# Rounding weight tiles one tile ahead, dealing whole tiles, and decay matrices by pairs of heads, in a hybrid DeltaNet and Conformer block

## The chip, the cores and the metric

The kernel runs on one core of one Trainium2 chip. The metric is the device time of one execution in microseconds, the median over several runs. The core has a matrix engine (PE; its weight loads are listed apart as PEld), VectorE (DVE), ScalarE (ACT), GpSimd (POOL) and SyncE (SP, which here issues most transfers). Each engine takes its instructions in a fixed order and waits at an instruction until the data of that instruction is there.

## The reference, cut to what matters

The block has 512 frames of width 1024, all in float32. One projection `h @ w_in` of the normalised input gives everything that the first stage needs: q, k, v and z of 8 heads of width 128, two small columns per head for the decay and for beta, the two halves of a gated linear unit, and two gates.

```python
h = rmsnorm(x, norm1_w[l])
proj = h @ w_in[l]
q, k, v, z, b_raw, a_raw, glu, gates = jnp.split(proj, SPLITS, axis=-1)
qkv = silu(causal_depthwise_conv(concat([q, k, v]), dn_conv_w[l]))     # 4 taps
q, k = l2norm(q), l2norm(k)
o = gated_delta_rule_chunked(q, k, v, g, beta)                         # per head
out_a = (rmsnorm(o, dn_norm_w[l]) * silu(z)) @ dn_w_o[l]
c = ga * sigmoid(gb)                                                   # glu
c = silu(layernorm(causal_depthwise_conv(c, cm_dw_w[l]) + cm_dw_b[l])) # 31 taps
out_b = c @ cm_w_pw2[l] + cm_b_pw2[l]
x = x + (sigmoid(gate_a) * out_a + sigmoid(gate_b) * out_b) @ w_out[l]
x = x + (silu(f_gate) * f_up) @ ffn_w_down[l]        # f_gate, f_up of rmsnorm(x)
```

The delta rule needs, for each head and chunk of frames, the matrix `decay = exp(gc_i - gc_j)` for j not above i and zero elsewhere, where `gc` is a running sum of the decay logarithms. It multiplies both `k k^T` and `q k^T`.

## The kernel before, in words

**Products.** Every float32 operand of a large product is split into two halves in PE's fast format, a rounded one and the rest. ACT makes the rounded one (`whi`, a copy, line 111) and DVE the rest (`wlo`, a subtraction, line 112). `split3` (line 121) then issues three matmuls for each 128 rows: `whi` with the high half of the activations, `whi` with the low half, and `wlo` with the high half. A weight tile is 128 x 1024; the product of one tile with all 512 frames takes 24 matmuls of 128 x 512 and gives one PSUM bank. `unit` (lines 101 to 113) loads a tile from memory over SP into `raw`, and makes `whi` and `wlo`; each of the three names has three buffers.

**The stage.** Of the 64 tiles of `w_in`, four are multiplied early. The other sixty run in a loop of generators. `proj(j)` (line 393) calls `unit` for tile j and then issues its eight groups of three matmuls, one group a step, into a bank of the pool `mm`, which has three. `head(h)` (line 793) runs the tiles 8+h (k), h (q), 16+h (v) and 24+h (z), 32 steps; head 0's k and q run interleaved in `proj2`, from tiles loaded before. For q, k and v, `conv4` (line 415) follows the tile: ACT scales the bank by the last tap into `acc` (line 419; the name `acc4` has two buffers), DVE adds three more taps (line 422), and ACT applies Silu (line 425) into `kT`, `qT` or `vT`. z goes through Silu straight from its bank (line 812). Between heads, `take(OTHERS[h])` runs so many steps of the other projections: `glu(i)` takes tile 40+i, a Sigmoid on ACT (line 677) and tile 32+i, for i from 2 to 7, and `gate(i)` takes tile 48+i and a Sigmoid (line 705). A tile is eight steps, so 12 steps are one and a half tiles. What is left of the others runs after the last head.

**Each head's recurrence.** `front` (line 451) transposes k, squares it on ACT, multiplies k by k, scales the result on ACT into `Un`, and multiplies it on POOL by the decay matrix `DT`; small blocks of that go through memory (`sc`, `U`) into a solve of thirty short POOL instructions. `front2` (line 507) transposes v and q and multiplies q by k; DVE multiplies that by `DT` into `at`. `chain` (line 529) finishes the inverse and runs over the four chunks of frames; it begins at a step of its own for each head, `START - 9 + 32 h + sum(OTHERS[:h])`, and is spread over some 65 steps beside the tiles of the next head.

**Decay matrices.** `decays` (line 773), traced at the third step of the loop, makes the running sums, with three small Exps, and stores a row per head and chunk in memory (`mrow`). `decay(*heads)` (line 438) does three things for each head: SP loads that row broadcast over 128 partitions into `DT` (four buffers, line 442), POOL adds a mask of large negative numbers (line 444), and ACT applies four Exps (line 449), one a chunk. It is called for head 0 in `decays`, for head 1 in head 0, and for heads 2 and 3, 4 and 5, 6 and 7 in heads 1, 3 and 5.

**What sets the order.** The framework's planner fixes the order of each engine's instructions before the run: at each point of its own forecast it takes, among those that it holds ready, the one that was traced first (the 31-tap convolution of the other branch, on DVE, ranks far behind and fills gaps). `tc.issue_after(i)` queues what its block traces on the engine of `i` behind `i`, in order alone. `marked` remembers the last instruction of a kind on each engine, `behind()` queues a block behind these marks, and both roundings of a tile are marked as "unit". The functions Silu, Sigmoid and Exp need different tables on ACT; a load of a table is placed by the compiler where the function changes, and shows as ACT_TABLE_LOAD under the line of the function that needs it.

From step 335 on, each call of `unit` also calls `fill`, which issues a part of the copies and sums that the FFN stage will read.

Of the kernel before, what the change touches and what calls it, by code (L numbers as in the profile page):

```python
# [6 lines left out]
F32 = mybir.dt.float32  # L7
F32R = mybir.dt.float32r
I32 = mybir.dt.int32
AF = mybir.ActivationFunctionType  # L10
ALU = mybir.AluOpType
# [3 lines left out]
P = 128  # L15
T = 512
NT = 4
D = 1024
KD = 8
H = 8  # L20
# [4 lines left out]
START = 78  # L25
ROUND = 40
WARM = 9
OTHERS = (12, 12, 12, 12, 8, 8, 8, 8)
EPS = 1e-6


# [1 line left out]
def block_kernel(ctx, tc, a):  # L33
    nc = tc.nc
    V, S, G, PE = nc.vector, nc.scalar, nc.gpsimd, nc.tensor
# [49 lines left out]
    def marked(b, kind="drain"):  # L85
        mark[b.ins.engine, kind] = b.ins
        return b
# [10 lines left out]

    last = [None]

    def unit(ap, pool=None):

        aps = ap if isinstance(ap, tuple) else (ap,)
        n = T * len(aps) if isinstance(ap, tuple) else 1024
        raw, hi, lo = ((pool or wp).tile([P, n if pool else 1024], t, name=x)[:, 0:n]
                       for t, x in ((F32, "raw"), (F32R, "whi"), (F32R, "wlo")))
        for i, p in enumerate(aps):
            loads.append(nc.sync.dma_start(raw[:, i * T:(i + 1) * T] if len(aps) > 1 else raw, p))
        if start_feed[0]:
            fill()  # L110
        marked(S.activation(hi, raw, AF.Copy), "unit")  # L111
        marked(V.tensor_tensor(out=lo, in0=raw, in1=hi.bitcast(F32), op=ALU.subtract), "unit")  # L112
        return hi, lo

    def split3(ps, wt, xh, xl, first, last, mv=False):

        wh, wl = wt
        terms = ((wh, xh), (wh, xl), (wl, xh))
        for i, (w, m) in enumerate(terms):
            l, r = (m, w) if mv else (w, m)  # L120
            marked(PE.matmul(ps, l, r, start=first and i == 0, stop=last and i == 2))  # L121
# [268 lines left out]
    def even_odd(t):  # L390
        return t.rearrange("p (q e) c -> p e q c", e=2)

    def proj(j):

        ps = psm.tile([P, T], F32, name="mm")
        hi, lo = unit(a["win"][j])
        for k in range(KD):
            s = slice(k * P, (k + 1) * P)
            if k:
                yield  # L400
            split3(ps, (hi[:, s], lo[:, s]), hh[:, k, :], hl[:, k, :], k == 0, k == KD - 1)
        return ps

    def proj2():

        both = [(psm.tile([P, T], F32, name="mm"), u) for u in first_two]
        for k in range(KD):
            s = slice(k * P, (k + 1) * P)
            for i, (ps, (hi, lo)) in enumerate(both):
                if k or i:  # L410
                    yield
                split3(ps, (hi[:, s], lo[:, s]), hh[:, k, :], hl[:, k, :], k == 0, k == KD - 1)
        return [ps for ps, _ in both]

    def conv4(j, name, ps=None):
        if ps is None:
            ps = yield from proj(j)
        acc = tp.tile([P, T], F32, name="acc4")
        S.activation(acc, ps, AF.Copy, scale=c4w[:, j, 3:4])  # L419
        for k in (2, 1, 0):  # L420
            s = 3 - k
            marked(V.scalar_tensor_tensor(out=acc[:, s:], in0=ps[:, :T - s], scalar=c4w[:, j, k:k + 1],  # L422
                                          in1=acc[:, s:], op0=ALU.mult, op1=ALU.add))
        o = gp.tile([P, NT, P], F32, name=name, bufs=1 if name == "vT" else 3)
        marked(S.activation(o.rearrange("p n t -> p (n t)"), acc, AF.Silu))
        yield
        return o

# [6 lines left out]
            PE.transpose(ps[:, n, :], src[:, n, :], ident)  # L435
        return ps

    def decay(*heads):

        for h in heads:  # L440
            DT = gp.tile([P, NT, P], F32, name="DT", bufs=4)
            nc.sync.dma_start(DT.rearrange("p n t -> p (n t)"),
                              mrow[h].rearrange("n t -> (n t)").partition_broadcast(P))
            G.tensor_tensor(out=DT, in0=DT, in1=neg.rearrange("p (a t) -> p a t", a=1).broadcast_to([P, NT, P]),
                            op=ALU.add)
            dts.append(DT)
        for h, DT in zip(heads, dts[-len(heads):]):
            for n in range(NT):
                S.activation(DT[:, n, :], DT[:, n, :], AF.Exp, bias=nmc[:, n, h:h + 1])

    def front(h, kT, DT):
        sq = junk[:, 0:P]
# [298 lines left out]
    def close():  # L751

        if ended and count[0] - ended[0][0] > ROUND - 8:
            if ended[0][1]:
                finish(*ended.pop(0)[2])
            else:
                scaled(*ended[0][2])
                ended[0][1] = True
# [14 lines left out]
    def decays():  # L773

        yield 2
        gps = psg.tile([P, 4, P], F32, name="g")
        fl = lambda t: t.rearrange("p n h -> p (n h)")
        for i, m in enumerate((tri, suf, ones, mid)):
            PE.matmul(gps[:, i, 0:32], m, fl(g), start=True, stop=True)
        S.activation(fl(egc), gps[:, 0, 0:32], AF.Exp)  # L780
        S.activation(fl(kdf), gps[:, 1, 0:32], AF.Exp)
        S.activation(fl(egl), gps[:, 2, 0:32], AF.Exp)
        V.tensor_scalar(out=negc, in0=egc, scalar1=-1.0, scalar2=None, op0=ALU.mult)
        V.tensor_scalar(out=fl(nmc), in0=gps[:, 3, 0:32], scalar1=-1.0, scalar2=None, op0=ALU.mult)
        mps = psg.tile([P, 4, P], F32, name="g")
        PE.matmul(mps[0:32, 0, :], fl(g), mid, start=True, stop=True)
        mr = mrt[0:32, 0:P]
        S.activation(mr, mps[0:32, 0, :], AF.Copy)
        for n in range(NT):
            nc.sync.dma_start(mrow[:, n, :], mr[n * H:(n + 1) * H])  # L790
        decay(0)

    def head(h, done):

        pk, pq = (yield from proj2()) if h == 0 else (None, None)
        k_ = yield from conv4(8 + h, "kT", pk)
        close()
        q_ = yield from conv4(h, "qT", pq)
        close()
        v = conv4(16 + h, "vT")  # L800
        for _ in range(2):
            next(v)
            yield
        DT = dts.pop(0)
        if h == 0 or h % 2 and h + 1 < H:
            decay(*range(h + 1, h + 3 if h else 2))
        with behind(), tc.issue_after(last[0].ins) if h else nullcontext():
            ss, kd, b2, Un, cp, y = front(h, k_, DT)
        v_ = yield from v
        pz = yield from proj(24 + h)  # L810
        z_ = zall[:, h, :]
        S.activation(z_, pz, AF.Silu)


        def second():
            Vp, at = front2(k_, q_, v_, DT, ss)
            done.append((h, k_, q_, ss, kd, b2, Un, cp, Vp, at, y, z_))
            yield 0

        chains.append([count[0] + 5, second()])  # L820
        yield
# [10 lines left out]
            yield  # L832


    done, ended, dts, convs, count, chains = [], [], [], [], [0], [[0, decays()]]
    rest = others()
    for h in range(H):
        queue.append(head(h, done))
# [241 lines left out]
    ff, made = [], []  # L1080
# [308 lines left out]
```

## Time and profile before

| | before |
|---|---|
| median of 3 runs | 942.55 us (942.53 to 944.67) |
| profiled execution | 943.44 us, its span 941.7 us |
| PE busy | 925.4 us, 98% of the span |
| DVE busy | 740.8 us, 79% |
| ACT busy | 558.0 us, 59% |
| POOL busy | 336.8 us, 36% |
| the loop of `proj` tiles | about 34 to 461 us |

Times in the profile are microseconds from the start of the span; in the groups of instructions the last number of a duration is the mean in ns. A line of a timeline gives the start, the duration, the engine and line, the operation, what it writes and reads, how many like it follow each other, and in brackets how long the engine had been idle and what ended that. Matmuls overlap, so their pace is read from one start to the next and not from the duration. A line of the table by stretches gives the stretch, its length, the busy time of PE, PEld, DVE, ACT and POOL with the count of instructions, the granted clock of PE as a share of the full one, and the transfers' share and rate.

### The profile page before, as it was taken

The numbers are of one execution on the slowest core, as the hardware profiler recorded it, in microseconds if no ns is written. First come the engines' busy times: TensorE is split into PE (matmuls) and PEld (weight loads), VectorE is DVE, ScalarE is ACT, GpSimd is POOL, SyncE is SP. The second block draws the span as 40 slices with busy tenths as digits, with TensorE's granted clock in tenths as the row PEclk, the third lists the DMA queues.
The fourth block names the chain that finished last, engine by engine and source line by source line (L and its number), as shares of the span: only waits on it lengthen the run. The fifth ranks groups of instructions, "written<-read, shape, count | busy, mean of one in ns | idle before, by whom it ended". The sixth has DMA issues, their size and how long they took to land.

```text
span 941.7 us, 14545 instructions
## 1 busy us (share of the span) xinstructions
PE 925.4 (98%) x4952; PEld 785.3 (83%) x4952; DVE 740.8 (79%) x1157; ACT 558.0 (59%) x1278; POOL 336.8 (36%) x541
## 2 busy tenths in 40 slices
PE   9999999999999999999999999999999999999996
PEld 6777788878888888888888888988889999988885
DVE  4889898989989899999587643676536877888896
ACT  6696977888778796643555323324324445466545
POOL 0134345253353437544055341245531111133042
PEclk9999999999999999999999999999999999999999
DMA  9333413223123246989898983699797564577654
GB/s 322 113 114 118 131 68 103 86 85 108 73 77 103 93 136 159 335 263 268 284 286 279 285 236 127 205 292 288 257 257 213 184 197 168 186 236 255 213 181 148
DMA packets 78187, 177.39 MB, mean 188 GB/s; under 512 B 10080, under 2 KB 19472, under 8 KB 77088
## 3 DMA queue, kind: packets, MB, share of 16 engines
q1 hardware_dynamic: 66528, 144.89, 44.9%
q0 software_dynamic: 10288, 28.90, 13.3%
q10 hardware_dynamic: 1296, 2.67, 0.7%
q8 instruction: 39, 0.64, 0.3%
q14 instruction: 36, 0.29, 0.1%
HBM read 156.22 MB, written 45.37 MB: 214 GB/s over the span
## 4 chain that ended last, share of the span: by engine, by line
PE 82%; ACT 7%; DVE 3%; issue 1%; POOL 1%; DMA 1%; POOLq 0%; ACTq 0%; DVEq 0%; SPq 0%
PE mm L121 55%; PE w L121 20%; PE b L526 2%; DVE wlo L112 1%; ACT whi L111 1%; PE g L435 1%; PE g L470 1%; PE st L639 1%; PE st L630 1%; PE st L638 1%; PE st L624 1%; PE st L625 0%; ACT Un L473 0%; DVE xs L964 0%; PE b L435 0%
## 5 line engine op out<-in xcount | busy, mean ns | idle before, releaser
L111 ACT ACTIVATE whi<-raw 128x1024 fp32r<-128x1024 f32 (+1 forms) x191 | 196.4, 1030 | 242.6 <-PE mm L121 158.0
L112 DVE TENSOR_TENSOR wlo<-raw,whi 128x1024 fp32r<-128x1024 f32 (+1 forms) x191 | 239.6, 1256 | 86.1 <-ACT whi L111 84.8
L121 PE MATMUL mm<-hh,whi 128*128 128x512 f32 (+1 forms) x688 | 269.7, 392 | 1.2 <-ACT whi L111 0.8
L121 PE MATMUL mm<-hh,wlo 128*128 128x512 f32 (+1 forms) x688 | 264.2, 385 | 0.8 <-DVE wlo L112 0.8
L121 PE MATMUL mm<-hl,whi 128*128 128x512 f32 (+1 forms) x688 | 263.0, 382 | 0.0
L693 DVE SCALAR_TENSOR_TENSOR cps<-c,c31w,cps 128x512 f32<-128x512 f32 x224 | 167.9, 749 | 3.8
L121 PEld LDWEIGHTS mm<-hh,wlo 128*128 128x128 f32 x688 | 130.0, 189 | 25.0 <-DVE wlo L112 1.3
L121 PEld LDWEIGHTS mm<-hh,whi 128*128 128x128 f32 x688 | 130.3, 189 | 22.9 <-ACT whi L111 1.7
L121 PEld LDWEIGHTS mm<-hl,whi 128*128 128x128 f32 x688 | 130.3, 189 | 20.9
L1022 POOL TENSOR_TENSOR fm<-fm 128x256 f32<-128x256 f32 x33 | 28.1, 852 | 117.7 <-DVE s L1022 93.2
L422 DVE SCALAR_TENSOR_TENSOR acc<-mm,c4w,acc 128x511 f32<-128x511 f32 (+2 forms) x72 | 53.0, 740 | 4.3 <-ACT acc L419 4.1
L502 POOL TENSOR_TENSOR ytm<-U,y 128x60 f32<-128x60 f32 (+14 forms) x120 | 36.7, 306 | 51.0 <-DMA U<-sc 42.2
L121 PE MATMUL mm<-yh,whi 128*128 128x512 f32 x128 | 50.6, 396 | 0.0
L121 PE MATMUL mm<-yh,wlo 128*128 128x512 f32 x128 | 49.8, 389 | 0.0
L121 PE MATMUL mm<-yl,whi 128*128 128x512 f32 x128 | 49.8, 389 | 0.0
L121 PE MATMUL w<-hh,wlo 128*128 128x256 f32 x168 | 47.7, 284 | 0.3 <-DVE wlo L112 0.3
L121 PE MATMUL w<-hh,whi 128*128 128x256 f32 x168 | 47.6, 284 | 0.0
L121 PE MATMUL w<-hl,whi 128*128 128x256 f32 x168 | 47.5, 283 | 0.0
L196 POOL DMA_DIRECT2D s<-in_wgu_dram x24 | 22.7, 962 | 64.0 <-DMA s<-in_wgu_dram 64.0
L121 PE MATMUL w<-wlo,fh 128*128 128x512 f32 (+1 forms) x115 | 44.3, 385 | 0.2 <-DVE wlo L112 0.2
L121 PE MATMUL w<-whi,fl 128*128 128x512 f32 (+1 forms) x115 | 44.2, 385 | 0.0
L121 PE MATMUL w<-whi,fh 128*128 128x512 f32 (+1 forms) x115 | 44.2, 385 | 0.0
(346 smaller groups left out, 1937.5 us busy)
## 6 DMA issues: line engine op xcount, KB each, us to landing
raw<-in_win_dram SPq DMA_DIRECT2D x61, 512.0 KB, 3.2
raw<-in_wgu_dram SPq DMA_DIRECT2D x32, 512.0 KB, 3.2
s<-in_wgu_dram SPq DMA_DIRECT2D x48, 256.0 KB, 5.3
raw<-s SPq DMA_DIRECT2D x48, 256.0 KB, 3.6
raw<-wsum SPq DMA_DIRECT2D x44, 256.0 KB, 3.6
raw<-in_wdn_dram SPq DMA_DIRECT2D x33, 256.0 KB, 3.2
s<-in_wgu_dram POOLq DMA_DIRECT2D x24, 256.0 KB, 6.8
s<-s POOLq DMA_DIRECT2D x24, 256.0 KB, 7.2
```

The costliest lines, as they stand in the source:

```text
L111: marked(S.activation(hi, raw, AF.Copy), "unit")
L112: marked(V.tensor_tensor(out=lo, in0=raw, in1=hi.bitcast(F32), op=ALU.subtract), "unit")
L121: marked(PE.matmul(ps, l, r, start=first and i == 0, stop=last and i == 2))
L196: fed.append(nc.gpsimd.dma_start(*begun.pop(0), accum_op=ALU.add, max_dma_last_dim=2048))
L422: marked(V.scalar_tensor_tensor(out=acc[:, s:], in0=ps[:, :T - s], scalar=c4w[:, j, k:k + 1], in1=acc[:, s:], op0=ALU.mult, op1=ALU.add))
L435: PE.transpose(ps[:, n, :], src[:, n, :], ident)
L470: PE.matmul(ps[:, n, :], kT[:, n, :], kT[:, n, :], start=True, stop=True)
L502: G.tensor_tensor(out=tm[:, :, 0:w], in0=U[:, k, :, k + 1:], in1=y[:, :, k:k + 1].broadcast_to([P, NT, w]), op=ALU.mult)
L526: PE.matmul(ps[:, q, 0:w], stationary[:, q, :], moving[:, q, :], start=True, stop=True)
L624: PE.matmul(ps[:, 0, :], kT[:, n, :], Sp, start=True, stop=True)
L693: V.scalar_tensor_tensor(out=acc if k < 30 else cv[i], in0=c[:, k:k + T], scalar=c31w[:, i, k:k + 1], in1=acc if k > 1 else cv[i], op0=ALU ...
L1022: return eng.tensor_tensor(out=out, in0=in0, in1=in1, op=op)
```

## The change: what it does

Three parts go together.

1. `proj(j)` no longer calls `unit` for its own tile. It takes the tile from `ready`, and after the first of its eight groups of matmuls it calls `ahead(j)`, which calls `unit` for the tile that follows. The order of all tiles is worked out beforehand in `tiles`. The roundings of a tile are still marked when its own `proj` begins (`later`). `proj2` calls `ahead` in its middle.
2. `OTHERS` goes from (12, 12, 12, 12, 8, 8, 8, 8) to (16, 8, 16, 8, 8, 8, 8, 8), so that only whole tiles are dealt between heads; the sums up to heads 2, 4 and later stay the same. The starting steps of the chains follow the same sums.
3. `decay` is split. `masked` loads the rows and adds the mask, for heads 0 and 1 in `decays` and for the next pair in heads 0, 2 and 4. `decay` issues the eight Exps of a pair: in `decays`, and in heads 1, 3 and 5 between the tracing of q and of v. The Exps are queued behind the last Silu of `conv4` traced before them, and each Silu of `conv4` behind the last Exp.

```diff
-OTHERS = (12, 12, 12, 12, 8, 8, 8, 8)
+OTHERS = (16, 8, 16, 8, 8, 8, 8, 8)
...
-    def unit(ap, pool=None):
+    def unit(ap, pool=None, later=None):
...
-        marked(S.activation(hi, raw, AF.Copy), "unit")
-        marked(V.tensor_tensor(out=lo, in0=raw, in1=hi.bitcast(F32), op=ALU.subtract), "unit")
+        made = S.activation(hi, raw, AF.Copy), V.tensor_tensor(out=lo, in0=raw, in1=hi.bitcast(F32), op=ALU.subtract)
+        if later is None:
+            for b in made:
+                marked(b, "unit")
+        else:
+            later.extend(made)
         return hi, lo
...
+    side = [t + i for i in range(2, KD) for t in (40, 32)] + [48 + i for i in range(16)]
+    tiles, done_ = [], 0
+    for h_, n_ in enumerate(OTHERS):
+        tiles += [8 + h_, h_, 16 + h_, 24 + h_] + side[done_ // 8:(done_ + n_) // 8]
+        done_ += n_
+    tiles += side[done_ // 8:]
+    follows, ready = dict(zip(tiles, tiles[1:])), {}
+
+    def ahead(j):
+
+        if j in follows:
+            marks = []
+            ready[follows[j]] = unit(a["win"][follows[j]], later=marks), marks
+
     def proj(j):
 
         ps = psm.tile([P, T], F32, name="mm")
-        hi, lo = unit(a["win"][j])
+        (hi, lo), marks = ready.pop(j)
+        for b in marks:
+            marked(b, "unit")
         for k in range(KD):
             s = slice(k * P, (k + 1) * P)
             if k:
                 yield
             split3(ps, (hi[:, s], lo[:, s]), hh[:, k, :], hl[:, k, :], k == 0, k == KD - 1)
+            if k == 0:
+                ahead(j)
         return ps
...
     def proj2():
...
+            if k == KD // 2:
+                ahead(0)
         return [ps for ps, _ in both]
...
-        marked(S.activation(o.rearrange("p n t -> p (n t)"), acc, AF.Silu))
+        with tc.issue_after(exps[0].ins) if exps[0] else nullcontext():
+            silu[0] = marked(S.activation(o.rearrange("p n t -> p (n t)"), acc, AF.Silu))
         yield
         return o
...
-    def decay(*heads):
+    def masked(*heads):
 
         for h in heads:
             DT = gp.tile([P, NT, P], F32, name="DT", bufs=4)
             nc.sync.dma_start(DT.rearrange("p n t -> p (n t)"),
                               mrow[h].rearrange("n t -> (n t)").partition_broadcast(P))
-            G.tensor_tensor(out=DT, in0=DT, in1=neg.rearrange("p (a t) -> p a t", a=1).broadcast_to([P, NT, P]),
-                            op=ALU.add)
+            a_ = G.tensor_tensor(out=DT, in0=DT, in1=neg.rearrange("p (a t) -> p a t", a=1).broadcast_to([P, NT, P]),
+                                 op=ALU.add)
             dts.append(DT)
-        for h, DT in zip(heads, dts[-len(heads):]):
-            for n in range(NT):
-                S.activation(DT[:, n, :], DT[:, n, :], AF.Exp, bias=nmc[:, n, h:h + 1])
+            raised.append((h, DT, a_))
+
+    silu, exps = [None], [None]
+
+    def decay():
+
+        with tc.issue_after(raised[-1][2].ins), tc.issue_after(silu[0].ins) if silu[0] else nullcontext():
+            for h, DT, _ in raised:
+                for n in range(NT):
+                    exps[0] = S.activation(DT[:, n, :], DT[:, n, :], AF.Exp, bias=nmc[:, n, h:h + 1])
+        raised.clear()
...
-        decay(0)
+        masked(0, 1)
+        decay()
...
         q_ = yield from conv4(h, "qT", pq)
         close()
+        if h % 2 and h + 1 < H:
+            decay()
         v = conv4(16 + h, "vT")
...
-        if h == 0 or h % 2 and h + 1 < H:
-            decay(*range(h + 1, h + 3 if h else 2))
+        if h % 2 == 0 and h + 2 < H:
+            masked(h + 2, h + 3)
...
```

More of the change, by code (lines that the diff above doesn't have):

```diff
@@ L832, in take @@
             yield
-    done, ended, dts, convs, count, chains = [], [], [], [], [0], [[0, decays()]]
+    raised, done, ended, dts, convs, count, chains = [], [], [], [], [], [0], [[0, decays()]]
     rest = others()
```

## The prediction

> **What bounds the kernel now.** I read the page first, then the chain of waits for PE's pace, then groups and timelines of PE, ScalarE (ACT) and GpSimd (POOL) for the stage that the change touches.
>
> ```profile
> span 941.7 us, 14545 instructions
> PE 925.4 (98%) x4952; PEld 785.3 (83%) x4952; DVE 740.8 (79%) x1157; ACT 558.0 (59%) x1278; POOL 336.8 (36%) x541
> ...
> 485.05 65.32 PE mm L121 x288
> ```
>
> PE is the bound. The last line, of the chain of waits in a stretch with nothing in PE's way, gives its pace: 65.32 / 288 = 0.227 us from one 128x512 matmul to the next. No edit takes a matmul away, so a gain can only be time in which PE runs slower than this. The profiled run took 943.44 us, 1.7 more than its span; the median of the runs is 942.55, and I apply differences to that.
>
> The changed loop (the `proj` tiles) lasts from about 34 to 461 us. Does PE wait there for rounded weights? The next lines are the rounding on ACT up to 446 us, and the first matmul of the stage behind the loop.
>
> ```profile
> L111 ACT ACTIVATE whi<-raw 128x1024 fp32r<-128x1024 f32 x60 | 63.4, 1058 | 45.3 <-PE mm L121 43.6 <-issue 1.2
> ...
> L121 PE MATMUL mm<-yh,whi x128: 389/389/791, 461.4 to 549.5; 128*128 128x512 f32 x128
> ```
>
> By 446 us all 60 tiles of the loop are rounded, but the 60th is multiplied only in the last 24 x 0.227 = 5.4 us before 461.4, from 456 on. So the rounding already runs some ten us ahead: it starts when PE frees a buffer (43.6 us of ACT's idle time end so). A one-tile lead in the trace order can help only where ACT was too full to use that freedom. PE's timeline shows one such place:
>
> ```profile
> 54.44 0.60 PE L435 MATMUL g<-cst,kT 128*128 128x128 f32 x4
> 54.88 1.06 PE L470 MATMUL g<-kT 128*128 128x128 f32 x8
> ...
> 64.44 0.39 PE L121 MATMUL mm<-hh,whi 128*128 128x512 f32 x1
> ...
> 66.25 0.39 PE L121 MATMUL mm<-hh,wlo 128*128 128x512 f32 x1
> 67.00 0.66 PE L435 MATMUL g<-cst,vT 128*128 128x128 f32 x4 [0.36 <-ACT vT L425]
> ...
> 69.31 0.39 PE L121 MATMUL mm<-hl,whi 128*128 128x512 f32 x1
> 70.03 0.66 PE L435 MATMUL g<-cst,qT 128*128 128x128 f32 x4 [0.33 <-DVE at L517]
> ...
> 72.61 0.39 PE L121 MATMUL mm<-hh,wlo 128*128 128x512 f32 x1
> 73.33 0.50 PE L121 MATMUL mm<-hh,whi 128*128 128x512 f32 x1 [0.34 <-ACT whi L111]
> ...
> 76.10 0.79 PE L121 MATMUL mm<-hh,wlo 128*128 128x512 f32 x1 [0.82 <-DVE wlo L112]
> ...
> 79.25 0.44 PE L121 MATMUL mm<-hh,whi 128*128 128x512 f32 x1
> ```
>
> From 72.61 to 79.25 PE starts 13 matmuls, 12 steps worth 2.7 us, in 6.64 us: **3.9 us lost** at tile 9, the k of head 1, whose halves `whi` and `wlo` come late. Part of it is the clock, in the stretches' table (PE, PEld, DVE, ACT, POOL busy, then the granted clock):
>
> ```profile
> 76.00:79.30 3.30, 3.20 (x8) 2.53 (x9) 3.27 (x5) 3.29 (x8) 2.78 (x4) 0.50 0.64 205
> ...
> 80.00:100.00 20.00, 20.00 (x96) 16.68 (x95) 17.78 (x28) 10.92 (x26) 6.84 (x26) 1.00 0.32 117
> 100.00:120.00 20.00, 19.24 (x99) 15.03 (x98) 17.07 (x34) 19.45 (x64) 10.20 (x24) 1.00 0.32 95
> ...
> 180.00:200.00 20.00, 19.53 (x110) 15.38 (x109) 16.80 (x36) 19.45 (x72) 12.17 (x28) 1.00 0.30 95
> ```
>
> PE ran 3.3 us at half clock after those waits; seven matmuls at twice 0.227 are some 1.4 of the 3.9. Two more waits on head 0's path stand before it: 67.00 - 66.25 - 0.23 = 0.5 and 70.03 - 69.31 - 0.23 = 0.5, together **1.0 us**.
>
> **The change part by part.** *Late weights, minus 3.9.* ACT's timeline at the start:
>
> ```profile
> 51.73 1.28 ACT L425 ACT_TABLE_LOAD   x1
> 53.02 0.63 ACT L425 ACTIVATE kT<-acc 128x512 f32<-128x512 f32 x1
> 53.56 0.62 ACT L425 ACTIVATE qT<-acc 128x512 f32<-128x512 f32 x1
> ...
> 54.22 0.68 ACT L419 ACTIVATE acc<-mm,c4w 128x512 f32<-128x512 f32 x1
> ...
> 59.10 1.28 ACT L449 ACT_TABLE_LOAD   x1
> 60.39 1.28 ACT L449 ACTIVATE DT<-DT,sm 128x128 f32<-128x128 f32 x4
> ...
> 62.44 1.28 ACT L449 ACTIVATE DT<-DT,sm 128x128 f32<-128x128 f32 x4 [0.77 <-POOL DT L444]
> ...
> 65.02 1.28 ACT L425 ACT_TABLE_LOAD   x1
> ...
> 72.22 1.06 ACT L111 ACTIVATE whi<-raw 128x1024 fp32r<-128x1024 f32 x1
> ...
> 77.25 3.33 ACT L449 ACTIVATE DT<-DT,sm 128x128 f32<-128x128 f32 x11
> ```
>
> Tile 9's rounding begins at 72.22, behind 20 us of head 0's work, when PE needs it at 72.8. It will be traced four steps earlier, still behind head 0's squares and the first Sigmoid, so its rank changes little. What helps is room: a hole opens on ACT ahead of 61 us (next edit), and the buffer, tile 24's, is free from 64.44 - 5.4 = 59.0, where tile 42 begins; the 11 Exps at 77.25 move on to head 1 and leave the roundings of tiles 1 and 17 alone. I take the whole 3.9; bounds 0 and 3.9.
>
> *The Exps of heads 0 and 1 first, plus 1.9 for minus 1.0.* `decays` is traced at the third step, the Silus of kT and qT at the sixteenth; `conv4` now queues each Silu behind the last Exp traced. So kT's Silu leaves 53.02 and stands behind eight Exps, which wait for POOL's mask:
>
> ```profile
> 58.29 1.29 POOL L444 TENSOR_TENSOR DT<-DT,cst 128x512 f32<-128x512 f32 x1 [10.92 <-DMA DT<-mrow]
> ...
> L422 DVE SCALAR_TENSOR_TENSOR acc<-mm,c4w,acc 128x511 f32<-128x511 f32 (+2 forms) x72 | 53.0, 740 | 4.3 <-ACT acc L419 4.1
> ```
>
> Two masks end at 58.29 + 2 x 1.29 = 60.9, eight Exps (two of the x4 rows, 2.5) at 63.4, the table load at 64.7: kT's Silu ends at 65.3, qT's at 65.9. Behind them stands v's `acc` of 54.22, since `acc4` has two buffers and k's and q's hold them until their Silus: it ends at 66.6, its three taps (0.74 each) at 68.8, and only then is v's PSUM bank free. The pool has three banks: v's, z's (its Silu is as late) and tile 42's. Tile 34 begins at 64.44 now and would need one of them: PE stands 68.8 - 64.4 = 4.4 us, less kT's products of 54.44 and 54.88, which fall into it (1.3): 3.1. With the cold clock of above, 1.4, it is 4.5. If z's Silu goes ahead of the Exps at 59.2, its bank is free in time and it is 0. The nearest rows, the two waits of 0.5 which this replaces, say 1.0. I take 1.9, about midway between 1.0 and 3.1.
>
> The Trainium skill, "TensorE: Matmul & The Clock Gate", Part 1, has the clock halve after about 3.4 us without work; by that rule two shorter pauses here would not cool it and the bound is 3.1. The trace differs: no gap between 72 and 76 us reached 1.3 us and the clock still fell to 0.50, so I keep 4.5.
>
> *Table loads and the odd heads, 0.* A switch between Exp and Silu costs ACT 1.28 us, and Exps are now strewn:
>
> ```profile
> L425 ACT ACT_TABLE_LOAD x9 | 11.5, 1283 | 2.7 <-DVE acc L422 2.5
> ...
> L449 ACT ACT_TABLE_LOAD x6 | 7.7, 1283 | 0.1
> ...
> 162.61 0.40 ACT L449 ACTIVATE DT<-DT,sm 128x128 f32<-128x128 f32 x1 [2.95 <-POOL DT L444]
> ...
> 95.47 0.62 ACT L425 ACTIVATE qT<-acc 128x512 f32<-128x512 f32 x1
> ...
> 101.91 0.65 ACT L425 ACTIVATE vT<-acc 128x512 f32<-128x512 f32 x1
> ...
> PE b L526 <- ACT m L597: 0.6, 2, 0.4
> ```
>
> A single Exp at 162.61 had a load for itself. At the start two loads go (51.73 or 65.02, and 59.10); later the Exps cause seven (the other five of the x6, and a Silu load behind two of the broken batches), and three blocks in heads 1, 3 and 5 will cause six: three fewer, 3.85 us of ACT. The last row says what ACT's lateness costs PE, 0.3 a wait: minus 0.9. Against it, the blocks land where ACT is full. Head 1 runs from q's Silu at 95.47 to v's at 101.91 and on into a stretch in which ACT is 97% busy (19.45 of 20); head 3's is the like stretch, 180 to 200. There come in two loads and eight Exps, 5.0 us; out goes one head's batch (a load and four Exps, 2.6): 2.4 us more, while the Exps leave 80 to 100, where ACT was half idle. If PE pays all of it three times: plus 7.2. Between minus 0.9 and plus 7.2 I take 0, nearest to the wait that the trace shows.
>
> The Trainium skill, "ScalarE: Activation LUTs", What ACT_TABLE_LOAD costs, gives about 2.66 us a switch with a drain. Here kT follows 1.29 us after its load starts. By the page the three loads would be 8.0 us of ACT; by the rows 3.85.
>
> *At nothing.* Whole tiles: tile 34's 24 matmuls ran without a break of tile 9 up to 72.6 already; the bounds are minus 0.5 and plus 0.5, one wait of above. The decay transfers and POOL masks are as many, earlier; the `issue_after` on a POOL add holds no ACT instruction. One call of `fill` is lost, as the unit traced at step 335 is the next one, which moves the copies for the FFN by a tile, 5.4 us:
>
> ```profile
> L192 SPq DMA_DIRECT2D s<-in_wgu_dram x48: 494/500/2543, 309.4 to 705.1; - x48
> ```
>
> They start at 309 and are read after 690 in the same order, which hides that.
>
> The sum: -3.9 - 1.0 + 1.9 + 0 = -3.0, so 942.55 - 3.0 = **939.6 us** (span 938.7, profiled run 940.4).
>
> **Rivals.** *A, more gain:* z's Silu slips in ahead of the Exps, PE never stands for a bank, and fewer loads pay: -3.9 - 1.0 - 0.9 = -5.8, 936.8. For it: ACT has nothing else between about 57 and 60.9. Against it: the Exps were traced earlier and go first when ready. *B, the rounding does nothing:* tile 9's weights stay behind head 0's work, which itself slides by 12 us, and the new wait is added: -1.0 + 1.9 = +0.9, 943.4. For it: the ten us of lead and the unchanged rank. Against it: the room. *C, slower:* in heads 1, 3 and 5 ACT becomes what PE waits for. Place: v's Silu behind the block, and the chain of the head before it. Price 2.4 each, 7.2 - 3.0 = +4.2, 946.8; it decides from about 1.9 us a head. For it: 97% busy. Against it: PE lost only about 0.8 us in 100 to 120 (19.24 of 20).
>
> **How the numbers follow.** Forecast 0.40 (own range 937.5 to 941.5), A 0.20, B 0.18, C 0.22. This kernel can tell 0.3%, 2.8 us, from no change. Faster: 0.24 of the forecast and A's 0.20, 0.44. Same: 0.16 of the forecast, 0.15 of B, 0.02 of C, 0.33. Slower: C's 0.20 and 0.03 of B, 0.23. The range goes from 936.0, below A by one wait, to 945.6, into C; about 0.2 lies outside.
>
> **What would show it.** Right: no half clock between 76 and 79, `whi` of tile 9 done before PE ends tile 34, kT's Silu near 65, 24 table loads instead of 27 for ACT. PE standing between 64 and 69 for more than 4.5 us, or waits for vT, `m` or `R` that grow behind the Exp blocks of heads 1, 3 and 5, would make the forecast wrong upwards; an undisturbed PE from 60 to 80, downwards.

## The result

The changed kernel takes 949.65 us in the median (945.67 to 952.88), the kernel before beside it 942.54 us (941.44 to 944.67). The ratio is **1.0069, interval 1.0045 to 1.0093**: slower by 0.7%. The forecast was 939.6 us with a range from 936.0 to 945.6, so the time lies above the range. Rival C comes nearest by its number, 946.8, but the ground that it gave, the blocks of Exps in heads 1, 3 and 5, accounts for some 2 of the 7.1 us at most; no rival named the call of `fill` or the new dealing.

### The profile after

The page of the changed kernel, as for the kernel before:

```profile
span 948.4 us, 14539 instructions
PE 927.1 (98%) x4952; PEld 784.5 (83%) x4952; DVE 736.6 (78%) x1157; ACT 558.0 (59%) x1277; POOL 334.1 (35%) x537
```

The span is 6.7 us longer with the same 4952 matmuls. The first matmul of the stage behind the loop tells on which side of the loop's end the time went (group of PE's matmuls of `yh`; behind the durations stand the starts of the first and the last):

```profile
L125 PE MATMUL mm<-yh,whi x128: 389/389/791, 463.2 to 551.4; 128*128 128x512 f32 x128
```

The loop ends at 463.2 instead of 461.4, 1.8 later. Behind it the old kernel needs 941.7 - 461.4 = 480.3, the new one 948.4 - 463.2 = 485.2: **4.9 us are lost behind the loop**, where the change edits nothing. The stretches' table of the new kernel (PE, PEld, DVE, ACT, POOL busy, then granted clock, transfers' share and rate) has the places:

```profile
60.00:80.00 20.00, 19.32 (x96) 15.46 (x94) 17.28 (x27) 18.33 (x44) 8.25 (x6) 1.00 0.34 115
...
700.00:760.00 60.00, 56.33 (x422) 53.63 (x421) 38.69 (x52) 24.38 (x34) 18.85 (x19) 1.00 0.82 234
```

The clock is 1.00 in both, the half clock at tile 9 is gone, and PE is idle for 3.7 us between 700 and 760. To compare stretches of different kernels I use one sum below, the **lost time**: the length of a stretch less its matmuls at their undisturbed pace (0.227 us for 512 columns, 0.120 for 256, 0.110 for narrow ones; the last is rough, so only differences between kernels count). By it:

| stretch, us | before | after | before with part 1 alone | with part 2 alone | with part 3 alone |
|---|---|---|---|---|---|
| 60 to 80 | 5.1 | 1.5 | 3.3 | 3.0 | 1.7 |
| 80 to 130 | 2.6 | 4.7 | 2.9 | 3.1 | 3.8 |
| 130 to 190 | 2.2 | 4.0 | 1.9 | 3.0 | 2.9 |
| 190 to 310 | 6.1 | 8.5 | 6.4 | 7.6 | 6.6 |
| 700 to 800 | 0.0 | 5.0 | -0.1 | 0.1 | 0.0 |

(The last three columns are the experiments below.) So the start of the loop did gain; the middle of the loop took it back and more; and the FFN stage lost 5.0 by itself.

The start, in ACT's timeline of the changed kernel:

```profile
58.45 1.28 ACT L848 ACT_TABLE_LOAD   x1
59.75 0.60 ACT L848 ACTIVATE A<-mm 128x512 f32<-128x512 f32 x1
61.20 1.28 ACT L481 ACT_TABLE_LOAD   x1 [0.85 <-DVE cps L726]
62.51 2.54 ACT L481 ACTIVATE DT<-DT,sm 128x128 f32<-128x128 f32 x8
65.06 1.28 ACT L450 ACT_TABLE_LOAD   x1
66.36 0.63 ACT L450 ACTIVATE kT<-acc 128x512 f32<-128x512 f32 x1
...
71.83 1.06 ACT L111 ACTIVATE whi<-raw 128x1024 fp32r<-128x1024 f32 x1
```

The eight Exps stand together in front of kT's Silu, as the prediction had it. But z's Silu (L848) went ahead of them at 59.75, so its bank was free and PE never stood for one. In 60 to 80 the view of waits names for PE only kT, 0.6 us.

The waits of PE over the whole loop, 34 to 462, the six longest (in total, times, longest):

```profile
PE g L460 <- ACT kT L450: 1.5, 2, 0.8
PE st L671 <- ACT R L668: 1.4, 3, 0.5
PE st L672 <- ACT R L668: 1.1, 1, 1.1
PE g L460 <- ACT Vp L545: 1.0, 2, 0.8
PE mm L125 <- ACT whi L111: 0.6, 1, 0.6
PE b L559 <- POOL ytm L535: 0.6, 1, 0.6
```

No single stall is behind the loss in the loop: it is made of waits of about a microsecond or less, on the small products of the heads' recurrences.

The FFN stage is different. POOL's timeline of the changed kernel:

```profile
697.24 0.88 POOL L200 DMA_DIRECT2D s<-in_wgu_dram  x1
704.67 7.14 POOL L176 TENSOR_TENSOR wst<-wst 128x512 f32<-128x512 f32 x4 [6.55 <-DMA wst<-in_wdn_dram]
...
712.69 0.88 POOL L200 DMA_DIRECT2D s<-s  x1
...
740.54 0.81 POOL L200 DMA_DIRECT2D s<-s  x1 [7.06 <-DMA s<-s]
```

and the last of these issues in the kernel before:

```profile
715.47 0.81 POOL L196 DMA_DIRECT2D s<-s  x1 [6.69 <-DMA s<-s]
```

L200 (L196 before) issues the accumulating copies that build the sums of the FFN's weights, `s`. From 697 to 712 none is issued, because POOL waits 6.55 us for a block of the down projection's weights (`wst`) and then adds it for 7.14 us. Such blocks of `wst` were four before and are five now (groups of transfers, before and then after: KB each, us to landing):

```profile
wst<-in_wdn_dram POOLq DMA_DIRECT2D x4, 1024.0 KB, 8.1
```

```profile
wst<-in_wdn_dram POOLq DMA_DIRECT2D x5, 1024.0 KB, 8.4
```

The blocks that the earlier stages prepare by halves are seven before and six after: the groups of transfers of `wsum` from `U` and `wsh` are x8 and x6 before, x7 and x5 after. Behind the fifth block the copies end 25 us later than before; counted from the end of the loop, 277.3 us instead of 254.1, 23 later. The FFN reads `s` as its weights; ACT's waits between 700 and 760, changed kernel and then before:

```profile
ACT whi L111 <- DMA raw<-s: 12.3, 5, 5.5
```

```profile
ACT whi L111 <- DMA raw<-s: 2.3, 1, 2.3
```

PE then waits for the roundings, five times and 3.8 us in all between 700 and 760, where the kernel before has no wait of PE; the longest, in PE's waits of the changed kernel:

```profile
PE w L125 <- ACT whi L111: 1.2, 1, 1.2
```

### The profile page after: what moved, and what is told of

It reads as the page before. It is cut to its first block, busy times and chain, and to the rows that moved or that the text cites. A ratio compares the mean times of both kernels' runs of the same rounds, so it can differ in the third digit from the quotient of the medians.

```text
span 948.4 us, 14539 instructions
## 1 busy us (share of the span) xinstructions
PE 927.1 (98%) x4952; PEld 784.5 (83%) x4952; DVE 736.6 (78%) x1157; ACT 558.0 (59%) x1277; POOL 334.1 (35%) x537
## 4 chain that ended last, share of the span: by engine, by line
PE 70%; ACT 13%; DVE 6%; DMA 3%; issue 2%; POOL 1%; SPq 0%; POOLq 0%; ACTq 0%; DVEq 0%
PE mm L125 46%; PE w L125 18%; DVE wlo L111 2%; ACT whi L111 2%; DMA raw<-s 2%; PE b L559 1%; ACT DT L481 1%; DVE cps L726 1%; DVE acc L446 1%; ACT L450 1%; PE st L672 1%; ACT s L577 1%; ACT L481 1%; PE g L460 1%; ACT Un L506 1%
## 5 line engine op out<-in xcount | busy, mean ns | idle before, releaser
L1058 POOL TENSOR_TENSOR fm<-fm 128x256 f32<-128x256 f32 x33 | 31.0, 940 | 96.9 <-DVE s L1058 74.9
L176 POOL TENSOR_TENSOR wst<-wst 128x512 f32<-128x512 f32 x20 | 34.4, 1722 | 30.2 <-DMA wst<-in_wdn_dram 29.1
```

The source lines that it names most:

```text
L176: G.tensor_tensor(out=o, in0=x, in1=y, op=ALU.add)
L1058: return eng.tensor_tensor(out=out, in0=in0, in1=in1, op=op)
```

## The experiments

Each is compared with the kernel before, timed on the same chip beside it; the median of that lay between 941.45 and 941.83 us. Besides the ratio I give the end of the loop (the first `yh` matmul, as above).

### e1_feed: give the lost call of fill back

`unit` runs one tile earlier now, so with the old threshold one call of `fill` is lost. This kernel is the changed one with

```diff
-        start_feed[0] = count[0] >= 335
+        start_feed[0] = count[0] >= 327
```

> The changed kernel with the FFN's copies begun one tile earlier (threshold step 327 instead of 335), so that the same tiles carry a call of fill as before the change. Theory 1 (the lost call of fill makes the copies late for the FFN): the stand of PE between 720 and 745 us, 5.0 us in the changed kernel, goes, and the time falls to about 944.5 us, with a smaller spread. Rival (the FFN stands because the stage before it ended later, or the transfers were slow in that run): the stand stays and the time is about 949.5.

Measured: 945.62 us (944.89 to 946.95), ratio 1.0040 (1.0028 to 1.0052). The loop ends at 462.9, 0.3 from the changed kernel's, and behind it lie 943.4 - 462.9 = 480.5 us, as before the change. The lost time of 700 to 800 is 0.1. The copies end 254.5 us behind the loop, as before the change (254.1); POOL's timeline:

```profile
717.37 0.81 POOL L200 DMA_DIRECT2D s<-s  x1 [7.11 <-DMA s<-s]
```

So the whole loss behind the loop is the one call. On the ratios it is 0.0069 - 0.0040, 2.7 us; in the two profiled executions 485.2 - 480.5 = 4.7. The changed kernel's own runs spread over 7 us, those of this one over 2; that the size of this loss differs from one execution to the next fits that, but only one execution of each was profiled.

### e4_before_late_feed: lose the call in the kernel before

```diff
-        start_feed[0] = count[0] >= 335
+        start_feed[0] = count[0] >= 343
```

> The kernel before, with the FFN's copies begun one tile later (threshold step 343): one call of fill fewer, nothing else. Theory 1: PE stands some 3 to 7 us in the FFN between 700 and 760 us, and the time is 945 to 950 us. The prediction's step (the copies have room enough): 942.5, no stand.

Measured: 942.77 us (941.37 to 946.64), ratio 1.0010 (1.0000 to 1.0020), below the 945 to 950 that was expected. The fifth block is there in POOL's queue, but PE lost only 0.25 us between 700 and 800. POOL's timeline:

```profile
696.17 6.35 POOL L172 TENSOR_TENSOR wst<-wst 128x512 f32<-128x512 f32 x4 [5.03 <-DMA wst<-in_wdn_dram]
...
731.67 0.81 POOL L196 DMA_DIRECT2D s<-s  x1 [6.06 <-DMA s<-s]
```

The block and the late copies are the same, the price is not. Behind its loop's end, 459.3, the last copy comes 272.4 us later here, and the stage is only just fed; in the changed kernel it comes 277.3 us later and PE loses 5 us. That these five microseconds make the difference is argued from two executions and not shown. This kernel also gives a second number: its loop is that of the kernel before up to step 335, and it ends at 459.3, not at 461.4. The profiled execution of the kernel before took about 2 us longer in its loop.

### e5_round_only, e6_deal_only, e7_decay_only: one part each

The kernel before with part 1 alone (the list of tiles worked out for the old dealing, threshold 327):

```diff
-        hi, lo = unit(a["win"][j])
+        (hi, lo), marks = ready.pop(j)
...
+            if k == 0:
+                ahead(j)
...
-        start_feed[0] = count[0] >= 335
+        start_feed[0] = count[0] >= 327
```

> The kernel before with the first part alone: tiles rounded one tile ahead, with the threshold at 327 so that the calls of fill stay. If the parts add, as the first four runs say (rounding +0.2, dealing +2.5, decay +1.2 us): within 1 us of the kernel before. The prediction's step (late weights at 72 to 79 us, up to 3.9 us, go with the lead): about 2 to 4 us faster, and no wait for whi at 73.

With part 2 alone:

```diff
-OTHERS = (12, 12, 12, 12, 8, 8, 8, 8)
+OTHERS = (16, 8, 16, 8, 8, 8, 8, 8)
```

> The kernel before with the second part alone, OTHERS at 16, 8, 16, 8, 8, 8, 8, 8. If the parts add: about 2.5 us slower, lost between 100 and 310 us. The prediction's step (whole tiles are worth nothing, within 0.5 us): no difference.

With part 3 alone:

```diff
...
-        decay(0)
+        masked(0, 1)
+        decay()
...
+        if h % 2 and h + 1 < H:
+            decay()
...
-        if h == 0 or h % 2 and h + 1 < H:
-            decay(*range(h + 1, h + 3 if h else 2))
+        if h % 2 == 0 and h + 2 < H:
+            masked(h + 2, h + 3)
```

> The kernel before with the third part alone, Exps by pairs of heads. If the parts add: about 1.2 us slower in all, as a gain at the start (PE's loss in 60 to 80 us falls to 1.5) and a larger loss of some 3 us in heads 1, 3 and 5. The prediction's step (the start costs 1.9 for 1.0): PE's loss in 60 to 80 rises instead.

Measured:

| | us | ratio | end of the loop |
|---|---|---|---|
| part 1, rounding ahead | 941.73 | 1.0001 (0.9991 to 1.0010) | 459.4 |
| part 2, whole tiles | 943.71 | 1.0024 (1.0016 to 1.0033) | 461.4 |
| part 3, decay by pairs | 941.47 | 0.9998 (0.9990 to 1.0007) | 459.2 |

**Part 1 alone does nothing that can be measured.** Tile 9's rounding starts at 72.53, where it was at 72.22 before, and PE waits for it as before. ACT's timeline, PE's, and the stretches' table of this kernel:

```profile
72.53 1.06 ACT L111 ACTIVATE whi<-raw 128x1024 fp32r<-128x1024 f32 x1
```

```profile
73.64 0.50 PE L125 MATMUL mm<-hh,whi 128*128 128x512 f32 x1 [0.33 <-ACT whi L111]
74.85 0.50 PE L125 MATMUL mm<-hh,whi 128*128 128x512 f32 x1 [0.47 <-ACT whi L111]
```

```profile
72.00:76.00 4.00, 3.20 (x13) 1.90 (x12) 3.87 (x5) 4.00 (x11) 1.84 (x1) 1.00 0.60 166
76.00:80.00 4.00, 4.00 (x19) 3.31 (x18) 3.96 (x4) 3.98 (x12) 3.52 (x6) 1.00 0.76 242
```

But nothing follows these two waits: the clock stays at 1.00, and 19 matmuls start in the four microseconds after them. In 60 to 80 the lost time is 3.3 instead of 5.1. Kernels e4 and e10, whose start is untouched, have 3.0 there too, and so have e6, e9 and e11, which deal other numbers of steps behind head 0. But e12, which deals there as e6 does, has 4.2: the late `wlo` comes again, without the half clock. PE's timeline and the stretches' table of e12:

```profile
75.56 0.50 PE L121 MATMUL mm<-hh,wlo 128*128 128x512 f32 x1 [0.74 <-DVE wlo L112]
```

```profile
76.00:80.00 4.00, 4.00 (x19) 3.28 (x18) 3.93 (x5) 3.99 (x12) 3.45 (x8) 1.00 0.80 225
```

So about 2 us of the time that the forecast took from this place are there in some executions only: of the seven profiled kernels that have neither part 1 nor part 3 there, the late `wlo` came in two, the kernel before and e12, and the half clock in the kernel before alone.

**Part 2 costs 2.3 us** (0.24%), and part of it is in waits that the kernel before hardly has; PE's waits from 60 to 310 in this kernel (`R` is scaled by ACT in the chain, `ytm` is POOL's solve):

```profile
PE st L638 <- ACT R L635: 1.8, 3, 0.7
PE st L639 <- ACT R L635: 0.9, 1, 0.9
...
PE b L526 <- POOL ytm L502: 0.7, 1, 0.7
```

**Part 3 gains at the start and gives it back.** In 60 to 80 it loses 1.7 instead of 3.0 to 3.3, so the Exps' place is what gained there, not the rounding. PE no longer waits for `whi` there, though this kernel has no lead; the only wait of PE from 60 to 80:

```profile
PE g L454 <- ACT kT L444: 1.0, 1, 1.0
```

With part 1 beside it (e3 below) the lost time there is 1.5: the lead adds 0.2 at most. From 80 to 310 part 3 loses 13.2 where part 1 alone loses 11.2.

The three ratios add up to 0.0001 + 0.0024 - 0.0002 = 0.0023, and with the lost call's 0.0029 to 0.0052 of the 0.0069.

### e2_old_decay and e3_old_deal: all but one part

The changed kernel with the threshold at 327, and part 3 undone (e2) or part 2 undone (e3, with the list of tiles worked out for the old dealing):

```diff
-        masked(0, 1)
-        decay()
+        decay(0)
...
-OTHERS = (16, 8, 16, 8, 8, 8, 8, 8)
+OTHERS = (12, 12, 12, 12, 8, 8, 8, 8)
```

> As the run before it, with the decay part undone: each head's Exps where the kernel before has them, no order between Silu and Exp. Theory 2 (the blocks of eight Exps and two table loads in heads 1, 3 and 5 cost PE about 4 us between 100 and 230): PE's loss in 100 to 230 falls from 11.6 us to about 7.5 and the time to about 940.5. Rival (the loss there comes from the new dealing or from the roundings that rank higher): it stays near 11.6 and the time near 944.5.

> As the first run, with OTHERS back at 12, 12, 12, 12, 8, 8, 8, 8 (tiles listed in the order in which they then begin). If the dealing is worth nothing, as the prediction has it: within 1 us of the first run, 944.5. If whole tiles shorten head 1 and 3 and so crowd ACT there: about 2 us faster than the first run.

Measured: without part 3 944.43 us, ratio 1.0025 (1.0013 to 1.0037); without part 2 943.1 us, ratio 1.0010 (1.0000 to 1.0021). Against e1's 1.0040, taking the dealing out is worth 0.0030, 2.8 us, near the 2 that e3 expected if short heads crowd ACT. The call and the dealing, each taken out, thus hold 0.0059 of the 0.0069; what is left, e3's 0.0010, has an interval that begins at nothing. Taking the decay part out is worth 0.0015, which is not clear of the noise of two ratios known to about 0.0012 each. It is also less than was expected of e2: the lost time from 100 to 230 falls from 11.3 us in e1 to 9.3 and not to 7.5, and the time is 944.4, as its rival had it, and not 940.5.

Put together from the single parts instead, the 0.0069 has a remainder of 0.0017, 1.6 us. Whether the parts cost more together than alone is not shown: the remainder comes from four ratios, each known to about 0.001, which leave it uncertain by about 0.002. In the profiled executions the parts nearly add up. From 80 to 310 part 2 alone loses 2.4 us more than e4, which has none of the three parts, part 3 alone 1.9 more, part 1 alone 0.2 less, and all three together (e1) 5.0 more.

### e8_start_only: the start of part 3 without its blocks

The kernel before, with the Exps of heads 0 and 1 in `decays` and each Silu of `conv4` behind the last of them; the later pairs stay where they were.

```diff
...
-        decay(0)
+        exps[0] = decay(0, 1)
...
-        if h == 0 or h % 2 and h + 1 < H:
-            decay(*range(h + 1, h + 3 if h else 2))
+        if h % 2 and h + 1 < H:
+            decay(h + 1, h + 2)
```

> The kernel before with one piece of the third part: the Exps of heads 0 and 1 together in the first batch, with the Silus behind them; the other heads' Exps where the kernel before has them. Theory 3 (this piece alone makes the gain at the start): PE's loss in 60 to 80 us falls from 3 to 5 us to about 1.5, and with no blocks in heads 1, 3 and 5 the kernel is about 2 us faster than before, 939.5 to 940. Rival (the gain at the start comes from the lead in rounding): no gain.

Measured: 947.92 us (946.58 to 949.73), ratio 1.0061 (1.0047 to 1.0074): slower, where 939.5 to 940 was expected. The start's gain is there, 1.5 lost in 60 to 80. From 100 to 130 it loses 9.2 (2.5 before). The table loads of ACT ahead of it (L426 for Silu, L450 for Exp), then PE's two longest waits from 100 to 130, then a row of the stretches' table:

```profile
88.03 1.28 ACT L426 ACT_TABLE_LOAD   x1
90.92 1.28 ACT L450 ACT_TABLE_LOAD   x1
92.64 1.28 ACT L426 ACT_TABLE_LOAD   x1
98.05 1.28 ACT L450 ACT_TABLE_LOAD   x1
100.79 1.28 ACT L426 ACT_TABLE_LOAD   x1
```

```profile
PE b L530 <- ACT m L601: 2.8, 1, 2.8
PE mm L121 <- ACT whi L111: 1.3, 1, 1.3
```

```profile
117.90:124.70 6.80, 5.88 (x14) 4.26 (x15) 6.76 (x9) 6.73 (x9) 5.78 (x14) 0.50 0.39 128
```

The Exps of later heads, free to run when their masks are ready, come in pieces between Silus, each with a load: those behind the loads of 90.92 and 98.05 are the 17th and 18th, by the count of four a head head 4's. The kernel before has one load between 84 and 114, at 87.10, where this one has six. Behind the two waits PE ran 6.8 us at half clock; an estimate of what that cost is half of its 5.88 busy us, 2.9. That the loads made the waits is argued from their place, not shown. With the Exps bound into blocks and the masks earlier (e7) the time is 941.47, some 6 us less than here.

### e9_whole_even and e10_twelve: other dealings

The kernel before with more steps between heads, whole tiles or not:

```diff
-OTHERS = (12, 12, 12, 12, 8, 8, 8, 8)
+OTHERS = (16, 16, 16, 16, 8, 8, 8, 8)
```

```diff
-OTHERS = (12, 12, 12, 12, 8, 8, 8, 8)
+OTHERS = (12, 12, 12, 12, 12, 12, 12, 12)
...
-        start_feed[0] = count[0] >= 335
+        start_feed[0] = count[0] >= 327
```

> The kernel before with OTHERS at 16, 16, 16, 16, 8, 8, 8, 8: whole tiles, but 48 steps for each of the first four heads, none with 40. Theory 4 (whole tiles cost nothing; the 2.3 us of the new dealing come from heads 1 and 3 having 8 steps of other tiles instead of 12, so that ACT and the chains crowd there): no slower than the kernel before, 940.5 to 942. Rival (a half-finished tile is what helps, as its matmuls are ready to be put where PE would wait): about 2 us slower, as the dealing alone was.

> The kernel before with OTHERS at 12 for all eight heads, and the threshold of the copies at 327, which keeps the number of their calls. Theory 4: four more steps for heads 4 to 7 take waits out of 230 to 350 us, and the time is 940 to 941.5. Rival (room per head is not what counts there): within 0.3% of before, with the same waits.

Measured: e9 955.78 us, ratio 1.0148 (1.0129 to 1.0167), and e10 956.12 us, ratio 1.0148 (1.0133 to 1.0163). Neither number was expected. Between 350 us and the loop's end they lose 12.6 and 13.0 us where the kernel before loses 1.8. PE's timeline of e9 and of e10:

```profile
412.44 0.66 PE L435 MATMUL b<-cst,o 128*128 128x128 f32 x4 [3.60 <-ACT s L608]
...
468.98 1.21 PE L435 MATMUL b<-cst,o 128*128 128x128 f32 x4 [1.79 <-ACT o L665]
```

```profile
360.58 0.79 PE L121 MATMUL mm<-hh,whi 128*128 128x512 f32 x1 [3.39 <-ACT whi L111]
```

```profile
359.20:365.90 6.70, 5.32 (x13) 4.07 (x14) 4.36 (x7) 4.33 (x8) 5.68 (x14) 0.50 0.47 132
```

The last row is from the stretches' table of e10. With 16 more steps of other tiles dealt between the heads their recurrences begin later, and the last `o` comes when hardly a tile is left to multiply: its matmuls start at 468.98 in e9 and 468.27 in e10, 2 us before the loop's end, and at 455.47 before, 6 us before it. That is only a part of the loss. In e10 some 6 of the 13 us go between 350 and 370, in a wait of 3.39 us for a rounding and the half clock beside it, and in e9 a wait of 3.60 us in a chain and the half clock behind it cost some 5. As a test of whole tiles they say little: from 100 to 310 the lost time is 11.8 in e9 and 10.8 in e10, against 10.8 before and 13.2 in e6.

### e11_short_first and e12_first_pair: where the dealing's cost lies

```diff
-OTHERS = (12, 12, 12, 12, 8, 8, 8, 8)
+OTHERS = (8, 16, 8, 16, 8, 8, 8, 8)
```

```diff
-OTHERS = (12, 12, 12, 12, 8, 8, 8, 8)
+OTHERS = (16, 8, 12, 12, 8, 8, 8, 8)
```

> The kernel before with (8, 16, 8, 16, 8, 8, 8, 8): whole tiles as in the change, with the two extra tiles behind heads 1 and 3 instead of 0 and 2. Theory 5, the time goes where a head is followed by eight steps only, as the recurrence of the head before it then has less of other products beside it: the lost time moves with the short heads, 100 to 130 us above 3.3 (before 2.5) and 130 to 160 us near 0.5, where the change's own dealing had 1.4; the whole is about 2 us slower than before, 943.5 to 944. Theory 6, any dealing by whole tiles costs, as the starts of the chains then fall on the boundary of a tile: 130 to 160 us keeps about 1.4, and the whole is 2.3 slower.

> The kernel before with (16, 8, 12, 12, 8, 8, 8, 8): whole tiles between heads 0 and 1 alone, the later ones as before. Theory 5 and theory 6 alike: the part of the loss before 190 us stays (130 to 160 us near 1.4 instead of 0.5) and the part behind it goes (190 to 310 us near 6.1 as before, not 7.6), so that about half of the 2.3 is left, 942.6 to 943. If the whole 2.3 stays, or nothing of it, the loss doesn't lie where the stretches put it and the reading by stretches falls.

Measured: e11 946.5 us, ratio 1.0049 (1.0036 to 1.0061), the loop's end 463.6; e12 942.29 us, ratio 1.0001 (0.9992 to 1.0010), the loop's end 460.1. In e11 the loss of 100 to 130 rises to 4.7, which fits a cost that goes with the short heads, but 130 to 190 loses 3.1 as in e6, which fits a cost of whole tiles; and the size is twice what either expected. Most of the rise is one wait, in PE's and POOL's timelines of e11:

```profile
108.59 0.60 PE L526 MATMUL b<-m,s 128*128 128x32 f32 x4 [2.95 <-POOL DT L444]
```

```profile
106.39 1.26 POOL L444 TENSOR_TENSOR DT<-DT,cst 128x512 f32<-128x512 f32 x1 [7.41 <-DMA DT<-mrow]
```

POOL reached the mask of the next decay matrix first and waited 7.41 us for its row, and the recurrence behind it on POOL waited too. In e12 130 to 160 loses 0.6, not 1.4: the loss that e6 has there is not a matter of heads 0 and 1 alone, although the steps up to there are dealt alike. So **neither reading stands**: with the first pair alone dealt by whole tiles there is no cost to measure. By the condition that e12's expectation set, the reading by stretches falls with them: none of the 2.3 is left, so they don't lie where the stretches of one execution put them. What is shown is that the cost of a dealing depends on all of it, and comes out as different waits: `R` and `ytm` in e6, the mask in e11. That the order which the planner makes is what carries it is argued. Why the change's own dealing costs 2.3 stays open beyond this.

## Why the prediction was wrong

By its own steps, in us:

| step | forecast | shown by the runs |
|---|---|---|
| late weights (part 1) | -3.9 | 0.0 (e5) |
| Exps first, at the start | -1.0 + 1.9 | about -1.5 (60 to 80 in e7) |
| table loads and odd heads | 0 | about +2 (80 to 310 in e7) |
| whole tiles (part 2) | 0 | +2.3 (e6) |
| one call of `fill` | 0 | +2.7 (e1) |
| remainder, not clear of the noise | none | +1.6 |

The right side adds up to 7.1, as does the measured difference, 949.65 - 942.54; the sum is no independent proof, since the last row is what the others leave, and the second and third are split by the lost time of one execution.

**The step that failed most plainly is "At nothing", for the call of `fill`.** It took the copies to be moved by one tile, 5.4 us, and took that to be hidden, since they are read only after 690. It missed what else the call does and what else stands in the queue. With one call less the earlier stages prepare one block of the down projection less, and the FFN stage has to load and add that block itself, on the same POOL queue that issues the copies: 6.55 us of waiting and 7.14 of adds ahead of all copies behind it. The forecast also looked at the first copy, which is early enough, and not at the last, which moved from 715.5 to 740.5.

The Trainium skill, "Perfetto Trace Analysis", in Tensor Engine Instruction (under Per-engine timelines), calls GpSimd's execution queue a strict FIFO. The trace agrees: no copy is issued during the 14 us in which the block of `wst` is waited for and added.

**"I take the whole 3.9"** failed twice. The lead by itself moves nothing: in part 1 alone the rounding's rank does not change, as the step itself said, and PE's two waits for `whi` stay (Rival B's reason). What took these waits away is the "room", and that came from the Exps' new place alone (e7), so it is in the next row of the table. And half of the 3.9 was hardly there to be gained, since it came from a late `wlo` that few executions have and from the half clock of the one profiled execution. A second execution of the same steps (e4) ends the loop at 459.3 instead of 461.4. That the two terms for the start, -3.9 and +0.9, still come to -3.0 where the lost time of 60 to 80 went from 5.1 to 1.5 is luck: the gain came by another term, and in part from that execution.

**"I take 1.9"** for the start had the order of z's Silu wrong; whether PE would otherwise have stood for the bank no run shows. The condition that the step named, "If z's Silu goes ahead of the Exps ... it is 0", is what happened (Rival A's mechanism). kT's Silu ended at 67.0, 1.7 behind the 65.3 worked out.

**"Between minus 0.9 and plus 7.2 I take 0"** for the odd heads: the range was right, and the direction was Rival C's. The groups of ACT show why few loads were saved (L450 and L848 are Silu, L481 Exp):

```profile
L450 ACT ACT_TABLE_LOAD x7 | 9.0, 1283 | 4.0 <-DVE acc L446 3.9
L481 ACT ACT_TABLE_LOAD x4 | 5.1, 1283 | 0.9 <-DVE cps L726 0.9
L848 ACT ACT_TABLE_LOAD x3 | 3.8, 1283 | 0.1
```

Exp has four loads instead of six, but Silu ten instead of nine: one saved where the forecast had three. C's price of 2.4 a head is not borne out: part 3 alone loses some 2 us from 80 to 310, over all three blocks.

The Trainium skill, "ScalarE: Activation LUTs", What ACT_TABLE_LOAD costs, gives about 2.66 us for a switch, a load and a drain. The trace of the changed kernel has the load, but not the drain as time of its own: the Exps of 62.51 start 1.31 us after their load at 61.20, and kT's Silu 1.30 after its own, which starts where the Exps end (62.51 + 2.54 = 65.05).

**"The bounds are minus 0.5 and plus 0.5"** for the whole tiles rested on the fact that tile 34 ran unbroken. It looked at the tile that moves, and not at the recurrences, whose starting steps follow the same sums; that the loss came there is argued from the waits for `R` and `ytm` in e6, and it is more than four times the bound.

## What to carry to other kernels

When an edit drops or shifts a call that does background work, list everything that the call does and what stands behind it on each queue, and follow the last item to its reader, not the first. Before a gain is taken from a stall in one profiled execution, look for a second execution with the same code, since a single stall of several microseconds may be that execution's own. A dealing of work has no price of its own in a schedule that a planner makes: three dealings of as many steps in all cost 2.3, 4.6 and 0.1 us (e6, e11, e12), so the one that is meant has to be timed.

## What the runs showed of the hardware

In the profiled execution of the kernel before, the clock of PE fell to 0.50 after waits of 0.34, 0.47 and 0.82 us; in e12, after waits of 0.34, 0.47 and 0.74 at the same place and with PE as busy (2.45 of the four microseconds from 72 to 76, 2.46 before), it stayed at 1.00. In part 1 alone, with 0.33 and 0.47 and without the third wait, it stayed at 1.00 too. Long waits don't settle it either: it fell beside waits of 2.84 (e8), 3.39 (e10) and 3.60 us (e9), and stayed at 1.00 from 104 to 115 us in e11, beside one of 2.95. What tells these apart the runs don't show. By the clock's records in the traces the half clock inside the loop lasted 3.41 us (before, e9) or 6.83 (e8, e10), and its starts in one execution lie a multiple of 3.41 apart: 117.91 and 943.94 in e8 are 242 times 3.413.

The last copy of `s` is no measure by itself of what late copies cost: with it 254, 272 and 277 us behind the end of the loop, PE lost 0.0 to 0.1, 0.25 and 5.0 us between 700 and 800, but in e11, with it at 258.4 and no call lost, 0.9.
